# A two-block transformer on one core: the 32 small experts of the last layer get 21 load buffers, a plain fp32 gather and a reordered last stretch

## The chip, the core and the metric

The kernel runs on one core of a Trainium2 chip. The metric is device microseconds of one launch, median of several runs. The clock of TensorE (PE) is granted in two levels, 2.4 and 1.2 GHz; the column PEclk of the views is the mean of a stretch as a share of the higher one. SP is the engine that issues nearly all loads from HBM.

## The reference, cut to what matters

256 tokens of width 1024 pass two blocks. The first has sliding-window attention with a feed-forward net, then a forgetting attention with an 8-expert layer. The second has a hybrid mixer and a hierarchical layer of 32 experts, each between a residual and a layer norm. The change lies in the second block, for the most part in its expert layer:

```python
x = layer_norm_2(DEEPNORM_ALPHA * x + hybrid_mixer(x, ...), ln1_w[l], ln1_b[l])
h = hier_moe(x, router_group_w[l], ..., expert_w_gate[l], expert_w_up[l], expert_w_down[l])
x = layer_norm_2(DEEPNORM_ALPHA * x + h, ln2_w[l], ln2_b[l])

def hier_moe(x, ...):          # 4 groups of 8 experts, the best 2 of the best group
    g_logits = xf @ router_group_w + router_group_b
    g_sel = jnp.argmax(g_logits, axis=-1)
    e_logits = (xf @ router_expert_w + router_expert_b).reshape(T, 4, 8)[g_sel]
    top_logit, top_local = lax.top_k(e_logits, 2)
    weight = p_group * jax.nn.softmax(top_logit, axis=-1)
    ...
    hid = silu(xb @ expert_w_gate[e]) * (xb @ expert_w_up[e])
    y[tok] += (hid @ expert_w_down[e]) * weight
```

Each expert has three matrices of 1024 x 256 in fp32, 1 MB each, so the layer reads 96 MB.

## The kernel before, in words

**The end of the mixer** (`hybrid`, L2333). Its last dense pieces are the projection `up(0)` of the RWKV branch (L2513 adds its product to `hm`), the transposes of `hm` with a split into `xh` and `xl`, and the product with `w_out`, done by `out_gemm` in four pairs of 512 KB loads. Dense weights come by L107 (`k.st`) into tiles `wr`; ScalarE (L123) and VectorE (L124) then split each into two fp32r parts in buffers `ws`. How many split buffers there are at that place is set by `room(0, 3, ...)`: six. Then the layer norm, and `moe2`.

**The loads of the experts** (`Long`, `k.long2`, L191). A load takes the buffer that was used longest ago, and is issued in the order gate, up, down of each group of four experts: twelve loads of 1 MB a group, eight groups. The last four down matrices are split into eight halves, so there are 100 loads. SP issues all of them in program order; hardware loads have eight semaphores, so at most eight are under way, and a further one waits for the oldest. Buffers: `LONG2 = (5, 8)` of its own, five before `w_out` and eight after it, and four tiles of the mixer that are dead by then (`rpar`, `hy0`, `hy1`, `rz`): 17 in all. The first nine loads are issued between the second and the third load of `w_out`, the next eight once the mixer's pools close.

**The expert layer** (`moe2`). The router (L2552 loads `xwr`) ranks and counts; L2623 (`places_of`) makes the one-hot matrix `OH` of 32 slots an expert. `gather(q)` collects the tokens of two groups at once: 32 matmuls of 256 columns, in fp32r, with `x` in a high and a low part (`xxth`, `xxtl`; L2594 subtracts). Then an `If` (L2663, L2664) stands for experts with more than 32 tokens; with this input it isn't taken. On every engine it is a branch, and SP's path around it waits until each of the eight load semaphores has come. Then, for each q of 8: gate matmuls (128x32 outputs, `bank_g<-wx,xgx`), `combine` of the group before (`bank_acc<-xy,xOT`), up matmuls, the product `xhid` (L2725), its transposes, down matmuls, and `xy` (L2753, L2754). At q = 0, `slot_gates` stands between gate and up. At q odd, `gather(q + 1)` follows the up matmuls. At q = 5, L2733 issues two loads that spread the norm vectors over all partitions (512 KB each). At q = 7 the residual (four fp32 matmuls of 512 columns into `bank_acc`, from an `x` that ScalarE had multiplied by alpha at L2662) stands between up and down. The down matmuls of q = 7 come in two column halves, each with its own `xy`, `combine` and statistics.

Of the kernel before, what the change touches and what calls it, by code (L numbers as in the profile page):

```python
# [158 lines left out]
class Long:  # L159
# [20 lines left out]
    def load(self, kept=0):  # L180

        while self.done < len(self.plan):
# [10 lines left out]
            self.done += 1  # L193

# [263 lines left out]
def out_gemm(k, key, hi, lo, order, ln, ready=(), need={}, last=4):  # L458
# [3 lines left out]
    for grp in [[q] for q in order[:-last]] + [order[-last:]]:  # L462
        yield from until(ready, *(need[q] for q in grp if q in need))
        final = grp[-1] == order[-1]
        ws = [w[0] for w in k.st.get(*((key, q) for q in grp), *(ln.keys if final else ()))]
        if final:
            ln.take(ws[-2:])
# [21 lines left out]
def leftover(k, x, xT, over, n, kf, up, down):  # L489
# [3 lines left out]
    with k.pool("rest") as pool, tc.For_i(0, n) as e:  # L493
        acc = [[k.bank("acc") for _ in range(2)] for _ in range(2)]
        for j in range(kf):
            ps = [k.t()[:, :T] for _ in range(2)]
            for p, src in zip(ps, up(e, j)):
                for a in range(0, KD, 4):
                    w = pool.tile([128, 4, 128], F32, name="ow", tag="ow", bufs=1)
                    nc.sync.dma_start(w, src[:, a:a + 4])  # L500
                    for q in range(4):
                        k.pe.matmul(p, w[:, q], xT[:, a + q], start=a + q == 0, stop=a + q == KD - 1)
            h = pool.tile([128, T], F32, name="oh", tag="oh", bufs=1)
            nc.scalar.activation(h, ps[0], AF.Silu)
            nc.vector.tensor_mul(h, h, ps[1])
            for m in range(2):
                v = pool.tile([128, 512], F32, name="ow", tag="ow", bufs=1)
                nc.sync.dma_start(v, down(e, j)[:, m * 512:m * 512 + 512])
                for tb in range(2):
                    k.pe.matmul(acc[tb][m], h[:, tb * 128:tb * 128 + 128], v, start=j == 0, stop=j == kf - 1)  # L510
        for tb in range(2):
            for m in range(2):
                r = x[:, tb, m * 512:m * 512 + 512]
                nc.vector.scalar_tensor_tensor(r, acc[tb][m], over[:, tb, ds(e, 1)], r, op0=OP.mult, op1=OP.add)
# [724 lines left out]
def moe1(k, A, x, alpha, before, br):  # L1239
# [3 lines left out]
    with ExitStack() as mo:  # L1243
# [8 lines left out]
        with ExitStack() as ro:  # L1252
# [85 lines left out]
            with tc.If(nv > CAP):  # L1338
                wi, wo = (A[n].rearrange("l e a b -> (l e) a b") for n in ("w_exp_in", "w_exp_out"))
                leftover(k, x, xT, over, NE, KF,  # L1340
                         lambda e, j: [wi[ds(e, 1), :, i * DFF + j * 128:i * DFF + j * 128 + 128].rearrange(
                             "o (k p) n -> (o p) k n", p=128) for i in range(2)],
                         lambda e, j: wo[ds(e, 1), j * 128:j * 128 + 128].rearrange("o p n -> (o p) n"))
# [989 lines left out]
def hybrid(k, A, x, before, scratch, extra):  # L2333
    nc, tc = k.nc, k.tc
    with ExitStack() as hy:
# [7 lines left out]
        r = Rwkv(k, A, yp, wide)  # L2343
        ready = set()
# [8 lines left out]
        with ExitStack() as pa:  # L2353
# [42 lines left out]
            def dense():  # L2396
# [4 lines left out]
                for i in range(3):  # L2401
                    yield from mb(1, i)
                late = iter(())
# [27 lines left out]
        with ExitStack() as pb:  # L2431
# [34 lines left out]
            def dense2():  # L2466
# [30 lines left out]
                yield from gate(0, gt)  # L2497
# [19 lines left out]
            og = out_gemm(k, "o2", xh, xl, list(range(8)), ln)  # L2517
# [21 lines left out]
def moe2(k, A, x, alpha, bias, out):  # L2539
    nc, tc = k.nc, k.tc  # L2540
    with ExitStack() as mo:
# [4 lines left out]
        OH = pool.tile([128, 2, NX, CAP2], F32R, name="xOH")  # L2546
        gate = pool.tile([128, 8], F32, name="xgate")
        own = pool.tile([128, 4], F32, name="xown")
        xth, xtl = (pool.tile([128, 2, D], F32R, name=n, tag=n, bufs=1) for n in ("xxth", "xxtl"))
        wr = pool.tile([128, KD, 4 + NX], F32, name="xwr")  # L2550
        for nm, a, n in (("group", 0, 4), ("expert", 4, NX)):
            nc.sync.dma_start(wr[:, :, a:a + n], dram(A[f"router_{nm}_w_2"], 0, [[n, 128], [128 * n, KD], [1, n]]))  # L2552
        k.long2.load()
        mo.enter_context(k.banks(g=2, t=2, acc=4))
        gx = pool.tile([128, KD, 256], F32, name="xgx")

        def gather(q):

            for a in range(0, KD, 2):
                p = k.t()  # L2560
                for j in range(a, a + 2):
                    for i, src in enumerate((xth, xtl)):
                        for tb in range(2):
                            w = src[:, tb].rearrange("p (c j) -> p j c", j=KD)[:, j]
                            k.pe.matmul(p[:, (j - a) * 256:(j - a) * 256 + 256], w,
                                        OH[:, tb, 4 * q:4 * q + 8].rearrange("p e s -> p (e s)"),
                                        start=i == 0 and tb == 0, stop=i == 1 and tb == 1)
                k.copy(gx[:, a:a + 2], p.rearrange("p (j s) -> p j s", j=2))

        with ExitStack() as ro:  # L2570
            rp = ro.enter_context(k.pool(name="m2r", bufs=1))
            tl = lambda shape, name: rp.tile(shape, F32, name=name)
            xT = tl([128, KD, T], "xxT")
# [5 lines left out]
            ln = LayerNorm(k, x, 1.0, "nx")  # L2579
            for tb in range(2):  # L2580
                if tb == 0:
                    nc.scalar.copy(xth[:, 0], x[:, 0])
                turn_half(k, x, xT, tb)
                if tb:
                    nc.scalar.copy(xth[:, 1], x[:, 1])
# [6 lines left out]
                if tb:  # L2592
                    for i in range(2):
                        nc.vector.tensor_sub(xtl[:, i], x[:, i], xth[:, i].bitcast(F32))  # L2594
# [32 lines left out]
            places_of(0, 8)  # L2627
# [5 lines left out]
            places_of(8, NX)  # L2633
# [27 lines left out]
            for tb in range(2):  # L2661
                nc.scalar.mul(x[:, tb], x[:, tb], alpha)  # L2662
            nv = nc.values_load(cnt[0:1, 0:1], min_val=0, max_val=T)  # L2663
            with tc.If(nv > CAP2):  # L2664
# [201 lines left out]
```

## Time and profile before

| | |
|---|---|
| median of 3 runs | 1883.89 us (1883.79 to 1885.23) |
| profiled execution | 1883.33 us, of which span 1881.6 us |
| PE busy | 92% of the span |
| mean granted clock | 0.966 |
| DMA | 515.95 MB, 274 GB/s mean |

The difference of 1.73 us between the profiled execution and its span lies around the span and is taken as fixed. The last 300 us, the end of the mixer and the expert layer, are read in stretches of 5 and of 20 us; the shares of the whole span say little about them.

### The profile page before, as it was taken

What the parts mean: (1) busy time and instruction counts of PE and PEld (TensorE: products, weight loads), DVE (VectorE), ACT (ScalarE), POOL (GpSimd) and SP (SyncE); (2) the same over time, 40 slices, a digit from 0 to 9 for tenths busy, and PEclk for the clock granted to TensorE, in tenths of its full rate; (3) what the DMA queues carried; (4) which work ended last, traced back from release to release, by engine and by line L of the source; (5) the groups of instructions that cost most, each with busy time, mean ns of one, the idle gap of its engine ahead of it and who ended that gap; (6) DMA issues with size and microseconds to landing.
All of it is one profiled execution on the core that took longest, in us unless ns stands there. A gap on an engine that the chain in (4) does not pass through costs nothing. (4 is left out here: it accounts for less than half of the span.)

```text
span 1881.6 us, 41532 instructions
## 1 busy us (share of the span) xinstructions
PE 1735.6 (92%) x18447; PEld 1199.3 (64%) x18447; DVE 721.0 (38%) x1147; ACT 453.4 (24%) x791; POOL 364.9 (19%) x621
## 2 busy tenths in 40 slices
PE   8989999899899999999999999989989998798676
PEld 7867888788645464646565555678767676564242
DVE  5557664654502020210202020357676666511102
ACT  5534444364200000000000101033353333221000
POOL 5410999310100000000000000064333331000000
PEclk9999999999999999999999999989999999999988
DMA  7515666535499999999999999755464236789996
GB/s 224 152 58 182 203 234 200 178 101 199 184 348 384 405 385 401 385 401 388 385 405 372 417 370 415 263 198 156 133 181 123 85 97 220 286 341 419 419 419 251
DMA packets 126478, 515.95 MB, mean 274 GB/s; under 512 B 20892, under 2 KB 49994, under 8 KB 88916
## 3 DMA queue, kind: packets, MB, share of 16 engines
q1 hardware_dynamic: 123012, 497.39, 70.4%
q0 software_dynamic: 3280, 15.83, 2.5%
q8 instruction: 147, 2.41, 0.5%
q14 instruction: 39, 0.32, 0.1%
HBM read 503.48 MB, written 7.87 MB: 272 GB/s over the span
## 5 line engine op out<-in xcount | busy, mean ns | idle before, releaser
L223 PE MATMUL bank_r<-wl,gx 128*32 128x352 f32 x6144 | 459.4, 460 | 2.6 <-ACTq L1338 2.6
L223 PE MATMUL bank_g<-ws,xh 128*128 128x256 f32 (+2 forms) x1440 | 392.0, 353 | 17.7 <-ACT ws L123 8.6
L223 PEld LDWEIGHTS bank_r<-wl,gx 128*32 128x32 f32 x6144 | 220.5, 110 | 234.8 <-issue 125.2
L124 DVE TENSOR_TENSOR ws<-wr,ws 128x1024 fp32r<-128x1024 f32 (+1 forms) x200 | 258.0, 1300 | 162.1 <-ACT ws L123 161.7
L223 PEld LDWEIGHTS bank_g<-ws,xh 128*128 128x128 f32 x1440 | 259.4, 197 | 58.0 <-ACT ws L123 9.5
L123 ACT ACTIVATE ws<-wr 128x1024 fp32r<-128x1024 f32 (+1 forms) x200 | 209.6, 1057 | 212.6 <-PE bank_g L223 108.8
L223 PE MATMUL bank_g<-ws,xl 128*128 128x256 f32 (+2 forms) x720 | 237.7, 346 | 3.6 <-DVE xl L354 3.4
L223 PE MATMUL bank_r<-wl,ehT 128*32 128x256 f32 x4224 | 231.4, 379 | 4.2 <-DVE ehT L1425 4.0
L223 PEld LDWEIGHTS bank_r<-wl,ehT 128*32 128x32 f32 x4224 | 161.2, 110 | 72.2 <-issue 8.9
L1424 DVE TENSOR_TENSOR eh<-eh,bank_r 128x352 f32<-128x352 f32 x48 | 22.9, 505 | 428.4 <-PE bank_r L223 427.8
L547 POOL TENSOR_TENSOR lnmv<-lnmv,neghalf 128x1 f32<-128x1 f32 x10 | 10.0, 998 | 828.1 <-DVE lnmv L546 828.1
L223 PEld LDWEIGHTS bank_g<-ws,xl 128*128 128x128 f32 x720 | 142.1, 197 | 18.5 <-DVE xl L354 5.2
L1447 ACT CAST ey<-bank_r 128x256 fp32r<-128x256 f32 x24 | 8.9, 373 | 415.4 <-PE bank_r L223 414.5
L223 PE MATMUL bank_g<-wx,xgx 128*32 128x256 f32 x784 | 78.6, 429 | 21.1 <-DMA wx<-in_expert_w_gate_dram 14.0
L1448 DVE TENSOR_TENSOR ey<-bank_r,ey 128x256 fp32r<-128x256 f32 x24 | 10.1, 424 | 165.0 <-ACT ey L1447 164.9
L1418 ACT ACTIVATE eh<-bank_r 128x352 f32<-128x352 f32 x48 | 22.3, 465 | 206.8 <-PE bank_r L223 201.7
L223 PEld LDWEIGHTS bank_g<-wx,xgx 128*32 128x32 f32 x784 | 35.7, 122 | 52.6 <-DMA wx<-in_expert_w_gate_dram 18.3
L631 POOL TENSOR_TENSOR aP<-aP,ast 128x512 f32<-128x512 f32 (+1 forms) x20 | 24.9, 1243 | 173.6 <-DVE ast L629 132.4
L223 PE MATMUL bank_g<-ws,hh 128*128 128x512 f32 x176 | 57.5, 399 | 0.0
L223 PE MATMUL bank_g<-ws,oh 128*128 128x512 f32 x128 | 44.5, 410 | 0.0
L1425 DVE STREAM_TRANSPOSE ehT<-eh 128x704 f32<-128x704 f32 x24 | 43.0, 1791 | 0.8
L564 POOL TENSOR_TENSOR lnmv<-lnmv,neghalf 128x1 f32<-128x1 f32 x2 | 1.1, 560 | 215.1 <-DVE lnmv L563 215.1
(714 smaller groups left out, 2230.2 us busy)
## 6 DMA issues: line engine op xcount, KB each, us to landing
wl<-in_w_exp_in_dram SPq DMA_DIRECT2D x128, 1408.0 KB, 8.7
wl<-in_w_exp_out_dram SPq DMA_DIRECT2D x64, 1408.0 KB, 8.5
wr<-in_w_in_dram SPq DMA_DIRECT2D x54, 512.0 KB, 3.9
wx<-in_expert_w_gate_dram SPq DMA_DIRECT2D x26, 1024.0 KB, 19.1
wx<-in_expert_w_up_dram SPq DMA_DIRECT2D x23, 1024.0 KB, 19.9
wr<-in_w_ffn_in_dram SPq DMA_DIRECT2D x44, 512.0 KB, 4.4
wx<-in_expert_w_down_dram SPq DMA_DIRECT2D x21, 1024.0 KB, 19.9
wr<-in_w_out_dram SPq DMA_DIRECT2D x24, 512.0 KB, 4.2
```

Of the source, the lines that this page charges most:

```text
L123: nc.scalar.activation(hv, v, AF.Copy)
L124: nc.vector.tensor_sub(lv, v, hv.bitcast(F32))
L223: self.nc.tensor.matmul(out, lhsT, rhs, start=start, stop=stop)
L547: nc.gpsimd.tensor_tensor(mv[:, 3:4], mv[:, 2:3], self.k.neghalf, op=OP.pow)
L564: nc.gpsimd.tensor_tensor(mv[:, 3:4], mv[:, 2:3], self.k.neghalf, op=OP.pow)
L631: e.tensor_mul(P[:, hs, :nk], P[:, hs, :nk], st[:, 3, hs].rearrange("p (h o) -> p h o", o=1).to_broadcast([128, 2, nk]))
L1418: nc.scalar.activation(h[:, g, s * H2:s * H2 + H2], pa[g][s], AF.Silu)
L1424: nc.vector.tensor_mul(v, v, pb[g][s])
L1425: nc.vector.transpose(hT[:, g], h[:, g].rearrange("p (r j) -> p j r", j=KF))
L1447: nc.scalar.copy(y[:, 0, g], ps[g])
L1448: nc.vector.tensor_sub(y[:, 1, g], ps[g], y[:, 0, g].bitcast(F32))
```

## The change

Buffers and the order of loads: `LONG2 = (1, 8, 8)`. One own buffer exists from the mixer's start and takes its load among those of `w_in`. Two tiles (`hy1`, `hy0`) take theirs in the middle of `gate(0)`, before the loads of `w_up_rwkv`. Then `rpar`, `rz` and eight own buffers come, one load for each call of `more()`, between the loads of `w_out`; eight more follow at the end of the mixer. That is 21. Split buffers at `w_out`: four (`room(0, 1, ...)`).

```diff
-            extra(k.part_y, wide, ("rpar", "hy0", "hy1", "rz"))
+            spare(wide, "rpar", "rz")
+            more = extra(k.part_y)
...
                     mm3(k, p, [(br[0][:, 2 * q + j, ts], br[1][:, 2 * q + j, ts], ws[2 * n + q][0][:, j], ws[2 * n + q][1][:, j])
                                for q in range(2) for j in range(2)], True, True)
+                    more()
...
-LONG2 = (5, 8)
+LONG2 = (1, 8, 8)
...
+        def extra(until):
+            k.long2.room(LONG2[1])
+            held.append(room(0, 1, until))
+
+            def more():
+                k.st.load()
+                k.long2.load(most=1)
+            more()
+            return more
```

On SP's queue, from the first load of `w_out` on (`wr<-in_w_out`), before; `wx`, `hy`, `rpar` and `rz` are buffers of expert loads:

```order
L107 DMA wr_15614<-in_w_out_dram 128x1024
L107 DMA wr_15631<-in_w_out_dram 128x1024
L191 DMA wx_15664<-in_expert_w_gate_dram 128x2048
L191 DMA wx_15666<-in_expert_w_gate_dram 128x2048
L191 DMA wx_15668<-in_expert_w_gate_dram 128x2048
L191 DMA wx_15670<-in_expert_w_gate_dram 128x2048
L191 DMA wx_15672<-in_expert_w_up_dram 128x2048
L191 DMA rpar<-in_expert_w_up_dram 128x2048
L191 DMA hy_15676<-in_expert_w_up_dram 128x2048
L191 DMA hy_15678<-in_expert_w_up_dram 128x2048
L191 DMA rz<-in_expert_w_down_dram 128x2048
L107 DMA wr_15687<-in_w_out_dram 128x1024
```

The same place now:

```order
L107 DMA wr_15623<-in_w_out_dram 128x1024
L107 DMA wr_15640<-in_w_out_dram 128x1024
L192 DMA rpar<-in_expert_w_gate_dram 128x2048
L192 DMA rz<-in_expert_w_up_dram 128x2048
L192 DMA wx_15677<-in_expert_w_up_dram 128x2048
L107 DMA wr_15684<-in_w_out_dram 128x1024
L107 DMA wr_15689<-in_w_out_dram 128x1024
L192 DMA wx_15704<-in_expert_w_up_dram 128x2048
L192 DMA wx_15721<-in_expert_w_up_dram 128x2048
L192 DMA wx_15745<-in_expert_w_down_dram 128x2048
L192 DMA wx_15769<-in_expert_w_down_dram 128x2048
L107 DMA wr_15787<-in_w_out_dram 128x1024
```

Nine expert loads stood between the second and third load of `w_out`; now three do, and four between the fourth and fifth.

The gather and what goes with it: `xp` holds `x` in plain fp32, permuted so that the weights of a gather are contiguous (two ScalarE copies in place of the two casts). `gather(q)` runs for each q, with 16 matmuls of 128 columns. The subtractions of L2594 and the multiplication of L2662 are gone; `places_of` makes the first four experts, not eight, ahead of `gather(0)`.

```diff
-            for a in range(0, KD, 2):
+            for a in range(0, KD, 4):
                 p = k.t()
-                for j in range(a, a + 2):
-                    for i, src in enumerate((xth, xtl)):
-                        for tb in range(2):
...
+                for j in range(a, a + 4):
+                    for tb in range(2):
+                        k.pe.matmul(p[:, (j - a) * 128:(j - a) * 128 + 128], xp[:, tb, j],
+                                    OH[:, tb, 4 * q:4 * q + 4].rearrange("p e s -> p (e s)"), start=tb == 0, stop=tb == 1)
...
             if q < 7:
-                if q % 2:
-                    gather(q + 1)
...
+                gather(q + 1)
+            if q == 6:
+                rest()
                 for tb in range(2):
                     for n in range(2):
-                        k.pe.matmul(acc[tb][n], k.ident, x[:, tb, n * 512:n * 512 + 512], start=False, stop=False)
+                        k.pe.matmul(acc[tb][n], identa, natural(tb)[:, 64 * n:64 * n + 64], start=False, stop=False)
```

`rest()` is the branch for experts with more than 32 tokens, now at q = 6; the residual follows it, with alpha in the identity `identa`. The norm vectors come as 32 bytes a partition each (`xrows`, two loads of 4 KB); at q = 7, between gate and up, 16 matmuls of 128 columns with four copies spread them over a spare expert buffer. `xhid`, `xhT` and `xOT` have one buffer, not two. The descriptor area of the software queue is set to 4096 bytes (`dynamic_dma_scratch_size=4096`).

On SP's queue, the end of the expert stream before (the `hy` and `rz` of 512 columns are halves of down matrices; the names with `out` are the store of the result):

```order
L191 DMA hy_17265<-in_expert_w_up_dram 128x2048
L191 DMA hy_17267<-in_expert_w_down_dram 128x2x512
L191 DMA rz<-in_expert_w_down_dram 128x2x512
L191 DMA wx_17312<-in_expert_w_down_dram 128x2x512
L191 DMA wx_17314<-in_expert_w_down_dram 128x2x512
L191 DMA wx_17316<-in_expert_w_down_dram 128x2x512
L191 DMA wx_17339<-in_expert_w_down_dram 128x2x512
L191 DMA wx_17341<-in_expert_w_down_dram 128x2x512
L191 DMA wx_17343<-in_expert_w_down_dram 128x2x512
L583 DMA out_dram<-x 128x512 x4
```

Now, up to the branch:

```order
L192 DMA wx_17081<-in_expert_w_up_dram 128x2048
L192 DMA wx_17083<-in_expert_w_down_dram 128x2x512
L192 DMA wx_17134<-in_expert_w_down_dram 128x2x512
L192 DMA wx_17136<-in_expert_w_down_dram 128x2x512
L192 DMA wx_17138<-in_expert_w_down_dram 128x2x512
L192 DMA wx_17140<-in_expert_w_down_dram 128x2x512
L2692 TENSOR_LOAD xcnt
L2692 ISA x2
L2694 COMPARE_AND_BRANCH
```

The branch stands on SP between the fifth and the sixth half; the last three halves follow behind its body.

## Rows read from the trace of the kernel before

**Rows 1.** Windows: us, busy by engine (instructions), PEclk, DMA share, GB/s.
```profile
1700.00:1720.00 20.00, 13.10 (x119) 4.88 (x121) 2.35 (x4) 1.96 (x3) 0.00 (x0) 0.92 1.01 418
1680.00:1880.00 200.00, 148.90 (x1226) 76.68 (x1218) 27.94 (x46) 18.52 (x32) 4.63 (x6) 0.90 0.93 383
```
**Rows 2.** Chain of waits in the expert layer: start, length, what.
```profile
1663.18 4.91 PE bank_g L223 x64
...
1694.92 19.24 DMA wx<-in_expert_w_gate_dram
...
1833.06 19.90 DMA hy<-in_expert_w_up_dram
1853.01 5.33 PE bank_g L223 x58
1858.33 3.63 PE bank_acc L223 x8
...
1867.13 1.90 PE bank_g L223 x16
```
**Rows 3.** Windows of 5 us around w_out and the first gate group.
```profile
1609.00:1614.00 5.00, 3.59 (x8) 2.39 (x9) 3.58 (x3) 4.13 (x5) 0.00 (x0) 0.50 0.59 209
1649.00:1654.00 5.00, 4.85 (x49) 4.21 (x52) 2.57 (x5) 1.93 (x3) 0.83 (x4) 1.00 0.38 154
```
**Rows 4.** Timeline of SP: start, length of issuing, instructions, count.
```profile
1589.89 23.31 SPq L107 DMA_DIRECT2D wr<-in_w_out_dram  x6
...
1632.85 24.24 SPq L191 DMA_DIRECT2D wx<-in_expert_w_up_dram  x4
...
1804.18 0.33 SPq L2733 DMA_DIRECT2D xxth<-in_ln_w_dram  x1
```
**Rows 5.** Timelines of DVE, ACT and PE around w_out: [idle before, and its releaser].
```profile
1583.51 4.63 DVE L124 TENSOR_TENSOR ws<-wr,ws 128x1024 fp32r<-128x1024 f32 x4 [1.65 <-ACT ws L123]
1609.27 1.06 ACT L123 ACTIVATE ws<-wr 128x1024 fp32r<-128x1024 f32 x1 [10.37 <-DMA wr<-in_w_out_dram]
1589.61 0.63 PE L227 MATMUL bank_t<-ident,hm 128*128 128x128 f32 x4 [2.95 <-DVE hm L2513]
1589.99 4.59 PE L223 MATMUL bank_g<-ws,hyr 128*128 128x512 f32 x12
1594.78 3.06 PE L223 MATMUL bank_g<-ws,hyr 128*128 128x512 f32 x12
1610.37 0.79 PE L223 MATMUL bank_g<-ws,xh 128*128 128x512 f32 x1 [5.81 <-ACT ws L123]
```
**Rows 6.** Timeline of PE: router, gather(0), first gate, slot_gates, the combine in q = 7.
```profile
1631.53 1.94 PE L223 MATMUL bank_g<-xxT,xwr 128*36 128x128 f32 x16
...
1644.04 0.73 PE L223 MATMUL bank_t<-xOH,xxth 128*128 128x256 f32 x2 [1.13 <-DVE xOH L2623]
...
1652.16 3.66 PE L223 MATMUL bank_g<-wx,xgx 128*32 128x256 f32 x64
1656.89 5.33 PE L223 MATMUL bank_t<-xG,xOH 128*128 128x4 f32 x32 [1.08 <-POOL xG L2659]
...
1848.25 2.14 PE L223 MATMUL bank_acc<-xy,xOT 128*128 128x512 f32 x8
```
**Rows 7.** DMA issues: count, KB each, median us from issue to landing.
```profile
wr<-in_w_in_dram SPq DMA_DIRECT2D x54, 512.0 KB, 3.9
...
sCX<-far POOLq DMA_DIRECT2D x2, 1280.0 KB, 8.7
```
**Rows 8.** The two branch lines: engine, operation, duration ns, first and last start.
```profile
L1338 PEldq COMPARE_BRANCH  x1: 3918/3918/3918, 510.5 to 510.5; - x1
L2664 SPq EVENT_SEMAPHORE  x8: 17/17/17, 1652.9 to 1653.4; - x8
```
**Rows 9.** Timeline of POOL: the last of six loads issued in a row, and its use.
```profile
1247.35 0.54 POOL L1628 DMA_DIRECT2D sm<-far  x1
1249.94 1.60 POOL L1752 COPY srho<-sm 128x512 f32<-128x512 f32 x1 [2.05 <-DMA sm<-far]
```

More of the change, by code (lines that the diff above doesn't have):

```diff
@@ L178, in add, with load @@
         self.plan.append((dram(w, off, [[pitch, 128], *rows]), part))
-    def load(self, kept=0):
-        while self.done < len(self.plan):
+    def load(self, kept=0, most=1 << 30):
+        until = min(self.done + most, len(self.plan))
+        while self.done < until:
             b = min(self.bufs, key=lambda b: b[2])
@@ L486, in out_gemm, with leftover @@
                     ln.add(tb, n, ps[tb][n])
-def leftover(k, x, xT, over, n, kf, up, down):
+def leftover(k, x, xT, over, n, kf, up, down, tile, tbs=(0, 1), tag="acc"):
     nc, tc = k.nc, k.tc
-    with k.pool("rest") as pool, tc.For_i(0, n) as e:
-        acc = [[k.bank("acc") for _ in range(2)] for _ in range(2)]
+    with tc.For_i(0, n) as e:
+        nt = 128 * len(tbs)
+        acc = [[k.bank(tag) for _ in range(2)] for _ in tbs]
         for j in range(kf):
-            ps = [k.t()[:, :T] for _ in range(2)]
+            ps = [k.t()[:, :nt] for _ in range(2)]
             for p, src in zip(ps, up(e, j)):
                 for a in range(0, KD, 4):
-                    w = pool.tile([128, 4, 128], F32, name="ow", tag="ow", bufs=1)
+                    w = tile(512, "ow").rearrange("p (k n) -> p k n", k=4)
                     nc.sync.dma_start(w, src[:, a:a + 4])
                     for q in range(4):
-                        k.pe.matmul(p, w[:, q], xT[:, a + q], start=a + q == 0, stop=a + q == KD - 1)
-            h = pool.tile([128, T], F32, name="oh", tag="oh", bufs=1)
+                        k.pe.matmul(p, w[:, q], xT[:, a + q, tbs[0] * 128:tbs[0] * 128 + nt],
+                                    start=a + q == 0, stop=a + q == KD - 1)
+            h = tile(nt, "oh")
             nc.scalar.activation(h, ps[0], AF.Silu)
@@ L2343, in hybrid @@
         r = Rwkv(k, A, yp, wide)
+        k.long2.room(LONG2[0])
         ready = set()
@@ L2402, in dense @@
                     yield from mb(1, i)
+                k.long2.load()
                 late = iter(())
@@ L2496, in dense2 @@
                     yield from up(1, n, *bm)
-                yield from gate(0, gt)
+                for i, _ in enumerate(gate(0, gt)):
+                    if i == 2:
+                        spare(wide, "hy1", "hy0")
+                    yield
             weave(k, dense2(), r.steps(*br), r.ahead(room), lat=LAT_B)
@@ L2545, in moe2 @@
         G = pool.tile([128, 2, NX], F32, name="xG")
-        OH = pool.tile([128, 2, NX, CAP2], F32R, name="xOH")
+        OH = pool.tile([128, 2, NX, CAP2], F32, name="xOH", tag="xOH", bufs=1)
+        rows = pool.tile([128, 2, KD], F32, name="xrows")
         gate = pool.tile([128, 8], F32, name="xgate")
         own = pool.tile([128, 4], F32, name="xown")
[L2549 to L2553, printed above, removed]
+        xp = pool.tile([128, 2, KD, 128], F32, name="xp")
+        ordered = lambda tb: x[:, tb].rearrange("p (c j) -> p j c", j=KD)
+        natural = lambda tb: xp[:, tb].rearrange("p j c -> p c j")
         mo.enter_context(k.banks(g=2, t=2, acc=4))
-        gx = pool.tile([128, KD, 256], F32, name="xgx")
+        gx = lambda q: x[:, q % 2].rearrange("p (j s) -> p j s", j=KD)
         def gather(q):
-            for a in range(0, KD, 2):
+            for a in range(0, KD, 4):
                 p = k.t()
-                for j in range(a, a + 2):
-                    for i, src in enumerate((xth, xtl)):
[L2563 to L2568, printed above, removed]
+                for j in range(a, a + 4):
+                    for tb in range(2):
+                        k.pe.matmul(p[:, (j - a) * 128:(j - a) * 128 + 128], xp[:, tb, j],
+                                    OH[:, tb, 4 * q:4 * q + 4].rearrange("p e s -> p (e s)"), start=tb == 0, stop=tb == 1)
+                k.copy(gx(q)[:, a:a + 4], p.rearrange("p (j s) -> p j s", j=4))
         with ExitStack() as ro:
@@ L2572, in moe2 @@
             tl = lambda shape, name: rp.tile(shape, F32, name=name)
+            wr = tl([128, KD, 4 + NX], "xwr")
+            for nm, a, n in (("group", 0, 4), ("expert", 4, NX)):
+                nc.sync.dma_start(wr[:, :, a:a + n], dram(A[f"router_{nm}_w_2"], 0, [[n, 128], [128 * n, KD], [1, n]]))
+            for i, nm in enumerate("wb"):
+                nc.sync.dma_start(rows[:, i], dram(A[f"ln2_{nm}_2"], 0, [[KD, 128], [1, KD]]))
+            k.long2.load()
             xT = tl([128, KD, T], "xxT")
```

110 lines of the change are left out of this document (67 added, 43 removed).

## The prediction

> **What bounds the kernel now.** I read the windows of the expert layer first, then the chain of waits, then windows of 5 us back to where the loads begin, then the timelines of SP and of the computing engines there. In the expert layer the transfers are the bound: from 1700 to 1720 us the DMA share is 1.01 at 418 GB/s, and PE is busy 148.9 of the 200 us from 1680 on [rows 1]. The chain says the same: from 1694.92 to 1853.01 it is one expert load after another, eight pieces, each about 19.9 us long [rows 2]. With eight loads under way that is 19.9 / 8 = 2.5 us for 1 MB. So whatever brings a load forward by 2.5 us, or takes 1 MB out of the stream, brings the end forward, as long as nothing else becomes late.
>
> The stream isn't full all the time. From 1649 to 1654 the DMA share is 0.38 [rows 3]. All 17 buffers are full there: SP begins its last four issues at 1632.85 and isn't through with them for 24.24 us [rows 4], since a buffer is free again only when the first gate matmuls end, at 1652.16 + 3.66 = 1655.8 [rows 6]. Two things therefore set the place of the stream: how much has landed when the first group releases buffers, and when that is. That time is set by the mixer's end. There the rows show four losses. PE waits 2.95 us for `hm`, because DVE is busy from 1583.51 for 4.63 us with splits of `w_out` that nobody needs yet. PE waits 5.81 us at 1610.37, since ACT waited 10.37 us for a `w_out` load, to 1609.27 [rows 5]; that load stood in SP's queue behind nine expert loads, and six loads took 23.31 us to issue [rows 4]. And after each wait the clock is low: 12 matmuls take 4.59 us, where the next 12 take 3.06 (1.5 us lost) [rows 5], and the window from 1609 has a granted clock of 0.50, the 1.2 GHz level [rows 3], where 3.59 us go into eight matmuls; I put that at about 2.0 us. Sum: 2.95 + 5.81 + 1.5 + 2.0 = 12.3 us.
>
> **The change, part by part.**
>
> *Order at `w_out`.* Three expert loads stand ahead of the third `w_out` load, not nine: 6 x 2.5 = 15 us less queue, more than the 5.81 us of waiting. With four split buffers in place of six, DVE has two splits fewer ahead of `hm`, half of 4.63 us, so 2.3 of the 2.95 us go and most of the rest with them. New waits come: a split may now only start when PE has read the buffer's last content. One conversion and its subtraction, 1.06 + 4.63 / 4 = 2.2 us [rows 5], lie open once, and I add 0.7 us for a second partly hidden one. So -12.3 + 2.9 = -9.4 us. Ends: none open, -12.3; each of the three later pairs open as far as its 2.2 us plus 0.3 of slow clock, -12.3 + 7.5 = -4.8.
>
> *The first gather.* Before, it runs from 1644.04 to 1652.16, 8.1 us, for two groups. Now 16 matmuls for one group. The nearest low row is the router's, fp32 with 128 columns: 1.94 us for eight (16 records), 0.243 each, so 3.9 us; but its weights have 36 columns. `slot_gates` has weights of 128 and 4 columns at the low clock, 5.33 / 16 = 0.33 us each [rows 6]; with 128 columns instead and all at the low clock I bound it by the sum, 0.33 + 2 x 0.243 = 0.82, so 13 us. I take 6.2 us, between and near the low end, as the clock is high when the gather begins: -1.9. The one-hot matrix for four experts and not eight and the missing subtraction give another -0.4. Ends: -4.6 and +4.5. Together with `w_out`: -11.7 us at the first release (1655.8 becomes 1644.1) and, with the same matmuls up to there, at the end of the first up matmuls (1663.18 + 4.91 = 1668.1 [rows 2] becomes 1656.4).
>
> *Buffers.* At the first release 21 loads have landed instead of 17: they end about 20 us (eight loads) after the mixer's pools close, which is before 1644. Four loads of the stream are gone from the time after it: 4 x 2.5 = -10.0 us. Working from the front: four more land by about 1657, 71 MB are left, 71 x 2.5 = 177.5 us; the last byte lands near 1835 to 1837.
>
> *Norm vectors.* The two spread loads, the first at 1804.18 in the full stream [rows 4], carry 1 MB: -2.5 us. Two loads of 4 KB early cost nothing that anyone waits for.
>
> *Early loads.* The one among the `w_in` loads and the two ahead of `w_up_rwkv` can delay a dense load behind them by 2.5 to 5 us. A dense load lands in 3.9 us [rows 7], and splits wait in buffers ahead of PE, so I take 0; the other end is +2.5.
>
> *The tail.* The end before is 1881.6 - 1853.01 = 28.6 us behind the last up load (call that landing L). The residual leaves it: -3.63 us [rows 2]. In exchange 16 row matmuls stand ahead of the last up matmuls, 6.2 us like the gather's 16; they begin when `combine` ends, at 1848.25 + 2.14 = 1850.4 [rows 6], 2.6 us before L. So the up matmuls start 3.6 us later, but with no wait ahead of them they run as the group at 1652.16 does, 3.66, not 5.33 us. The second half of the down matmuls then wants to start at 1867.13 - 1853.01 = 14.1, minus 3.6, plus 3.6, minus 1.7: L + 12.4. Its weights come hardly sooner: SP's way round the branch waits for all eight semaphores, as the eight events of L2664 show before [rows 8], and only then issues three halves. The fifth half lands at about L + 5.2, the first of the three 3.9 us later [rows 7], the others 1.2 us apart: L + 11.5, within an us. So PE is last, at 12.4, and from there to the end it is 1881.6 - 1867.13 = 14.5 us as before: 26.9 instead of 28.6, -1.7 us. With the row matmuls at the low clock (6.2 us more) it would be +4.5.
>
> *At q = 6* the branch, the gather and the residual stand between up and down. The other branch of this form, L1338, cost PE 3.9 us [rows 8]; with 6.2 and 3.6 us that is 13.7 us beside a period of 12 x 2.5 = 30 us, of which PE uses about 22 (148.9 / 200 of it). Some 8 us are hidden, and the down buffers have the reserve of four more loads, 10 us. I take 0, and +5 as the other end.
>
> *The small area* for software descriptors I take at 0; its other end is rival 3.
>
> Sum: -9.4 - 2.3 - 10.0 - 2.5 - 1.7 = -25.9. From the profiled execution, 1883.33 us, which is 0.6 us under the median: **1857.4 us**.
>
> The Trainium skill, "DMA: Bandwidth & Descriptors", section "Specifications", gives about 358 GB/s as what HBM gives one core, which would be 2.9 us for 1 MB. The trace doesn't agree, with 418 GB/s over a whole window; by the page the five saved megabytes would be worth 14.6 us, not 12.5, and the sum -28.0. The measured rate stands.
>
> **Rivals.**
>
> 1. *`w_out` gains nothing.* Four split buffers put ACT, DVE and PE in line, and what the queue gives back is lost at the splits. For it: each of the four pairs needs two conversions and two subtractions, 4.5 us, not far from PE's own work on a pair, 24 matmuls of 3.06 / 12 us [rows 5], 6.1 us. Against: they run beside it as long as a buffer is free. Then -16.5: 1866.8 us.
>
> 2. *The work at q = 6 and the row matmuls are on the path.* PE has a slow clock in waits, the branch costs more than 3.9, and the release of buffers slips: +5, and 6.2 in the tail: 1868.6 us.
>
> 3. *Slower: the software queue.* POOL issues six loads in a row from 1244.60, the last at 1247.35, and the second of them is used 2.05 us later [rows 9]. If the smaller area holds one at a time, POOL waits for a landing between each two: 5 x 6.3 = 31.5 us, with 6.3 between the two landings of [rows 7]. It decides above 25.9 us, so nearly all of it would have to reach the end. Then 1857.4 + 31.5 = 1888.9. For it: POOL works half of that stretch and others wait for it. Against: no row shows POOL waiting for room, and 128 pieces a load are little.
>
> The Trainium skill has the area at 16 KiB a partition ("SBUF — State Buffer", section "SBUF size: 192, 224, or 256?") and nine descriptors a side and engine for 1 MiB, of 16 bytes ("DMA: Bandwidth & Descriptors", sections "The descriptor swizzle" and "Terms"); an estimate from that is 6 x 9 x 16 = 864 bytes for the six, inside 4096. No run here shows it.
>
> 4. *It doesn't do what it says.* The stream begins earlier but some later wait pins it, for instance buffers that PE releases too late for 21 to help; the new gather after each up at q even (6 us more there) could do that. Then only small gains remain, some 3 us: 1880.
>
> **How the numbers follow.** Forecast 0.58, its own range 1850 to 1865 (the ends of `w_out` and of the gather, not both at once). Rival 1 0.17, rival 2 0.11, rival 3 0.08, rival 4 0.06. The range 1850 to 1870 takes in the forecast and rivals 1 and 2; it leaves out rivals 3 and 4 and 0.05 of the others. A measurement of this kernel tells 0.2%, 3.8 us, from no change. Faster: 0.58 + 0.17 + 0.11 = 0.86. Within: rival 4, 0.06. Slower: 0.08.
>
> **What would show it.** PE's wait before `hm` and the 5.81 us at the first `w_out` pair gone, and the end of the `w_out` matmuls near 1620 (1629 before). First gate matmuls ending near 1644, `gather(0)` of 5 to 7 us. DMA share 1.0 from about 1657 to 1835. Eight semaphore events of SP in the last 25 us, then three halves; the residual ahead of the last group. It is wrong if the end of `w_out` stays near 1629 (rival 1), if PE is late with down at q = 6 (rival 2), if the start of the mixer moves (rival 3), or if the DMA share has holes after 1660 (rival 4).

## The result

The changed kernel takes 1860.88 us (median of 4 runs, 1858.82 to 1866.05), the kernel before 1883.84 us; the ratio is 0.9882, with a 95% interval of 0.986 to 0.9905. That is 23.0 us less; 25.9 us less were forecast, and the time lies inside the range of 1850 to 1870.

The profiled execution took 1866.05 us, the longest of the four, with a span of 1864.3 us. Where that matters below, the profile of a kernel that differs in its last three loads alone (`e2_loads_first`) stands beside it.

### The profile page after: what moved, and what is told of

Same layout as the page of the kernel before. It is cut to its first block, busy times and chain, and to the rows that moved or that the text cites. A ratio compares the mean times of both kernels' runs of the same rounds, so it can differ in the third digit from the quotient of the medians.

```text
span 1864.3 us, 41874 instructions
## 1 busy us (share of the span) xinstructions
PE 1730.8 (93%) x18607; PEld 1197.5 (64%) x18607; DVE 718.0 (39%) x1147; ACT 455.7 (24%) x791; POOL 363.9 (20%) x622
## 5 line engine op out<-in xcount | busy, mean ns | idle before, releaser
L232 PEld LDWEIGHTS bank_r<-wl,ehT 128*32 128x32 f32 x4224 | 161.2, 110 | 72.2 <-issue 8.9
L232 PE MATMUL bank_g<-wx,x 128*32 128x256 f32 x784 | 71.2, 433 | 15.6 <-DMA wx<-in_expert_w_gate_dram 14.4
L232 PEld LDWEIGHTS bank_g<-wx,x 128*32 128x32 f32 x784 | 32.7, 123 | 45.6 <-DMA wx<-in_expert_w_gate_dram 19.1
```

The source lines that it names most:

```text
L232: self.nc.tensor.matmul(out, lhsT, rhs, start=start, stop=stop)
```

## The profile after

**End of the mixer and first loads.** The timeline of SP, which answers to [rows 4]: start, length of issuing, count.

```profile
1578.08 1.47 SPq L107 DMA_DIRECT2D wr<-in_w_out_dram  x2
...
1585.15 1.46 SPq L107 DMA_DIRECT2D wr<-in_w_out_dram  x2
...
1597.69 3.74 SPq L107 DMA_DIRECT2D wr<-in_w_out_dram  x4
...
1627.60 19.71 SPq L192 DMA_DIRECT2D wx<-in_expert_w_down_dram  x2
```

The third `w_out` load goes out at 1585.15, and the last four need 3.74 us; before, six needed 23.31 us. The timelines of PE and DVE there, which answer to [rows 5]:

```profile
1583.89 2.36 DVE L124 TENSOR_TENSOR ws<-wr,ws 128x1024 fp32r<-128x1024 f32 x2 [1.65 <-ACT ws L123]
```
```profile
1587.72 0.63 PE L236 MATMUL bank_t<-ident,hm 128*128 128x128 f32 x4 [0.68 <-DVE hm L2540]
1588.11 3.04 PE L232 MATMUL bank_g<-ws,hyr 128*128 128x512 f32 x12
...
1596.45 0.50 PE L232 MATMUL bank_g<-ws,xh 128*128 128x512 f32 x1 [1.63 <-ACT ws L123]
...
1597.71 1.02 PE L232 MATMUL bank_g<-ws,xh 128*128 128x512 f32 x2 [0.53 <-DVE ws L124]
...
1622.98 0.60 PE L236 MATMUL bank_t<-ident,x 128*128 128x128 f32 x4
```

DVE has two splits ahead of `hm`, not four; the wait for `hm` is 0.68 us instead of 2.95, and the 12 matmuls behind it take 3.04 instead of 4.59. The wait of 5.81 us is gone. New are 1.63 and 0.53 us at the first `w_out` pair: the split buffers are still in use, as the text had charged. The transposes at 1622.98 mark the end of the `w_out` matmuls; before, they stood at 1629.16.

**First group and the hole in the stream.** PE's timeline of the changed kernel, then of `e2_loads_first`: `gather(0)` and `slot_gates`, which answer to [rows 6].

```profile
1637.94 5.44 PE L232 MATMUL bank_t<-xOH,xp 128*128 128x128 f32 x32 [0.86 <-DVE xOH L2651]
...
1648.32 6.24 PE L232 MATMUL bank_t<-xG,xOH 128*128 128x4 f32 x32 [1.35 <-POOL xG L2687]
```
```profile
1640.43 3.81 PE L232 MATMUL bank_t<-xOH,xp 128*128 128x128 f32 x32 [0.86 <-DVE xOH L2651]
...
1649.18 3.73 PE L232 MATMUL bank_t<-xG,xOH 128*128 128x4 f32 x32 [1.35 <-POOL xG L2687]
```

The same instructions take 5.44 and 6.24 us in the one execution, 3.81 and 3.73 us in the other. The granted clock differs with them. Windows of the changed kernel, then of `e2_loads_first`: columns as in [rows 1], PEclk third from the end.

```profile
1639.00:1644.00 5.00, 5.00 (x41) 4.62 (x43) 2.84 (x5) 0.53 (x1) 0.30 (x2) 0.66 1.02 423
1644.00:1649.00 5.00, 3.65 (x62) 2.22 (x55) 0.23 (x2) 3.77 (x9) 2.58 (x12) 1.00 0.44 143
1649.00:1654.00 5.00, 5.00 (x27) 5.00 (x26) 0.00 (x0) 0.00 (x0) 0.29 (x1) 0.52 0.99 411
1654.00:1659.00 5.00, 5.00 (x43) 2.82 (x47) 1.07 (x3) 0.00 (x0) 0.00 (x0) 0.50 0.92 387
1659.00:1664.00 5.00, 5.00 (x63) 3.87 (x56) 0.42 (x1) 0.59 (x1) 0.00 (x0) 0.96 0.37 116
```
```profile
1640.00:1645.00 5.00, 4.57 (x48) 4.20 (x52) 3.18 (x6) 0.65 (x2) 0.00 (x0) 1.00 1.01 419
1645.00:1650.00 5.00, 3.65 (x64) 2.25 (x52) 0.55 (x6) 3.65 (x8) 3.01 (x13) 1.00 0.76 280
1650.00:1655.00 5.00, 5.00 (x47) 3.98 (x50) 1.07 (x3) 0.00 (x0) 0.15 (x1) 0.80 1.02 424
1655.00:1660.00 5.00, 5.00 (x69) 3.12 (x62) 0.42 (x1) 0.00 (x0) 0.00 (x0) 0.86 0.95 385
```

In the changed kernel's profile the granted clock is 0.66 during the gather and 0.52 and 0.50 from 1649 to 1659, the 1.2 GHz level; in the other it is full during the gather. PE idles 1.35 us ahead of `slot_gates` in both, so that stretch alone doesn't explain the difference, and no run shows what does. In the ten other profiles that have the new gather, `gather(0)` takes 3.81 us: the changed kernel's own profile is the exception.

The holes in the stream, a DMA share of 0.44 and 0.37, answer to the 0.38 of [rows 3]. They are still there with 21 loads landed, the first one 5 us earlier. With the full clock they are small: 0.76, then 0.95.

**The tail.** PE's timeline, which answers to the end of [rows 2]:

```profile
1815.57 7.25 PE L232 MATMUL bank_acc<-xp,xidenta 128*128 128x512 f32 x8 [4.66 <-PEq L2694]
...
1832.62 1.95 PE L232 MATMUL bank_t<-ident,xrows 128*128 128x128 f32 x16
1834.84 2.05 PE L232 MATMUL bank_t<-ident,xrows 128*128 128x128 f32 x16 [0.27 <-ACT xgb L332]
...
1848.17 1.05 PE L232 MATMUL bank_g<-wx,xhT 128*32 128x512 f32 x2 [0.56 <-DMA wx<-in_expert_w_down_dram]
1849.48 1.90 PE L232 MATMUL bank_g<-wx,xhT 128*32 128x512 f32 x10 [0.27 <-DMA wx<-in_expert_w_down_dram]
```

The last transfer in the chain of waits (start, length):

```profile
1842.36 7.08 DMA wx<-in_expert_w_down_dram
```

The two branch rows that answer to [rows 8]:

```profile
L2694 SPq EVENT_SEMAPHORE  x8: 17/17/17, 1837.9 to 1840.9; - x8
L2694 PEldq COMPARE_BRANCH  x1: 6032/6032/6032, 1809.2 to 1809.2; - x1
```

PE idles 4.66 us behind the branch, the residual takes 7.25 us where it took 3.63, and the up matmuls start right behind the row matmuls, with no wait for weights. SP is through with its eight events at 1840.9. The first three of them, at 1837.9, 1839.2 and 1840.5, stand until the third, fourth and fifth half have landed (1837.8, 1839.2 and 1840.5); the other five follow within 0.4 us. Then SP issues the last three halves, at 1841.00, 1841.71 and 1842.36; the last of them lands 7.1 us later, and PE's last down matmuls wait for it to 1849.48.

## A yardstick for the runs

Between executions the whole program shifts: the first 12-matmul piece of `up(0)` starts at 1580.00 before and 1580.11 after, but anywhere from 1575.5 to 1584.0 in the eleven profiles that have the new order. Times of single stages are therefore counted from that start, and the tail from the issue of the first half load, which the stream alone sets (eight loads are under way, so it goes out when an earlier load lands).

| profile | up(0) starts | end of w_out | first gate | end of first up | first half issued | end, from that issue |
|---|---|---|---|---|---|---|
| before | 1580.00 | +49.2 | +72.2 | +88.1 | +255.5 | 46.1 |
| after | 1580.11 | +42.9 | +63.2 | +80.9 | +236.3 | 47.9 |
| e2_loads_first | 1583.97 | +41.5 | +60.2 | +74.6 | +229.9 | 45.2 |
| e3_17_buffers | 1580.47 | +41.4 | +60.1 | +74.5 | +239.6 | 48.3 |
| e7_loads_in_a_row | 1578.08 | +53.0 | +71.7 | +86.0 | | |

All of it is worked out from the timelines of PE and SP. The changed kernel's row has the low clock of its own profile in it. How far a single profile can be trusted in the last column, programs with the same or nearly the same tail show: the two variants of the kernel before (without its branch, and with the small descriptor area) have 44.5 us there, not 46.1, and the changed kernel and the five variants that keep its tail have 46.7 to 48.3. The first two rows of the last two columns give the result of the profiled executions: -19.2 up to the first half, +1.8 behind it, +0.1 ahead of `up(0)`, -17.3 in all, the difference of the spans.

## The experiments

**The branch left out.**

```diff
             if q == 6:
-                rest()
```

> The changed kernel without the branch at q = 6: the path for experts with more than 32 tokens is left out, all else stays. Theory A (PE is late at the end, because of the 4.66 us that it idles behind the branch and of a residual of 7.25 us at the low clock just behind it, and the three last halves are late by SP's way round the branch): the up matmuls of q = 7 wait for their weights again, the residual takes about 3.7 us, the last halves are there when the second half of the down matmuls starts; 5 to 8 us less than the changed kernel, 1853 to 1856. Theory B (the work at q = 6 is hidden behind the stream and only the late halves cost): 3 us less, about 1858.

1855.88 us (ratio 0.9837, 0.9812 to 0.9862), 5 us under the changed kernel. PE's timeline shows that the residual stayed long:

```profile
1807.98 7.10 PE L232 MATMUL bank_acc<-xp,xidenta 128*128 128x512 f32 x8
...
1820.70 0.40 PE L232 MATMUL bank_g<-rpar,x 128*32 128x256 f32 x1 [0.72 <-DMA rpar<-in_expert_w_gate_dram]
```

The window of the residual, columns as in [rows 1]:

```profile
1808.00:1815.00 7.00, 7.00 (x11) 1.71 (x10) 0.00 (x0) 0.59 (x1) 0.00 (x0) 1.00 1.01 421
```

With a granted clock of 1.00 it takes 7.10 us, and 7.25 in the changed kernel with 0.70, so the low clock was not the reason, against theory A. What differs from the residual before is the read: `natural(xp)` steps 128 elements from column to column, where `x` was contiguous. The weights are new as well (`identa` in place of the plain identity), and no run separates the two. The rest went as A has it: with the 4.66 us gone, PE waits again (0.72 us) at the gate of q = 7, and the end comes 42.9 us after the issue of the first half, not 47.9.

**The last halves ahead of the branch.**

```diff
             if q == 6:
+                k.long2.load()
                 rest()
```

> The changed kernel with its last three half loads issued ahead of the branch on SP, nothing else. Both theories: the second half of the down matmuls no longer waits; it started at 1849.48 and PE was through with the work before it at 1847.6, and it ran with gaps; 2 to 3 us less, 1858 to 1859. If the halves weren't the last thing waited for: no change.

1859.92 us (0.9874, 0.9841 to 0.9907). The medians don't separate 1 us; the profile does: the end is 45.2 us behind the first half's issue instead of 47.9, and no wait for a half is left in PE's timeline. So SP's way round the branch costs 2.7 us by this pair of profiles, 1.5 to 3.1 against all six with that tail (46.7 to 48.3).

**17 buffers.**

```diff
-LONG2 = (1, 8, 8)
+LONG2 = (1, 8, 4)
...
-                    gb = k.long2.spare([128, 2, D], "xgb")
+                    gb = ep.tile([128, 2, D], F32, name="xgb")
```

> The changed kernel with 17 buffers (four own ones fewer at the last stage) and a tile of its own for the spread norm vectors, so that only the buffers differ. Theory A: four loads of 1 MB come back into the stream behind the first release, 4 x 2.5 = 10 us, of which the 3.5 us that PE was late at the last up matmuls absorb a part: 6 to 10 us more, 1867 to 1871. Theory C (the gain is the earlier first release alone, buffers don't matter): no change.

1870.35 us (0.9937, 0.9912 to 0.9962), 9.5 us over the changed kernel. The stage up to the first gate is the same as with 21 (+60.1 and +60.2), and the first half is issued at +239.6 instead of +229.9: 9.7 us for four loads, 2.4 each (8.3 to 10.2 us against `e2_loads_first` and the four other variants with 21 buffers that keep the loads in between and the residual at q = 6). Theory C falls, and the lateness of PE absorbs nothing that shows. One more thing differs: with 17 buffers the branch stands on SP between the first and the second half, so seven halves go out behind it, not three; the last column of the table, 48.3 us, hardly shows it.

**Six split buffers.**

```diff
-LONG2 = (1, 8, 8)
+LONG2 = (1, 6, 10)
...
-            held.append(room(0, 1, until))
+            held.append(room(0, 3, until))
```

> The changed kernel with six split buffers at w_out, as before, and the buffers of the experts as six there and ten after it, 21 as in the changed kernel. Theory A: PE's 1.63 and 0.53 us of waiting at the first w_out pair and the low clock behind them (about 2.5 us) go, but DVE has four splits ahead of hm again (2.3 us): the end of the w_out matmuls near 1621 instead of 1623, 0 to 2 us less in all. If the split buffers are what made the gain at w_out smaller than forecast: 4 us less.

1860.53 us (0.9886, 0.9855 to 0.9917): no change.

```profile
1585.20 0.63 PE L236 MATMUL bank_t<-ident,hm 128*128 128x128 f32 x4 [2.95 <-DVE hm L2540]
```

(Two of the experts' own buffers also come later in this kernel.) The wait of 2.95 us for `hm` is back to the hundredth, and the 1.63 and 0.53 us at the first pair are gone; the end of `w_out` is at +41.1 instead of +41.5. The two numbers of split buffers trade one wait for another.

**Loads in a row at `w_out`.**

```diff
             def more():
                 k.st.load()
-                k.long2.load(most=1)
+                k.long2.load()
```

> The changed kernel with the ten expert loads at w_out issued in a row, between its second and third load, as before; buffers, split buffers and all else as changed. Theory A (the interleaving is what shortens the end of the mixer): the third w_out load stands behind 10 MB again, 25 us; PE waits 6 to 9 us in the middle of w_out and has the low clock after it, the end of the w_out matmuls is 7 to 10 us later and with it the end: 1866 to 1870. Theory F (the fewer splits ahead of hm did it, the transfers are hidden): no change.

1869.01 us (0.9926, 0.9897 to 0.9955), 8.1 us over the changed kernel. In PE's timeline:

```profile
1611.24 0.80 PE L232 MATMUL bank_g<-ws,xh 128*128 128x512 f32 x1 [7.83 <-ACT ws L123]
```

The stall before, 5.81 us, returns as 7.83, with ten loads ahead of `w_out` where there were nine. The end of `w_out` is at +53.0 instead of +41.5. So the interleaving makes the end of the mixer shorter; theory F falls.

**The residual spread over q = 2 to 5**, with the halves first. The branch's body clears `xp` and adds the residual of its own results.

```diff
-                for tb in range(2):
-                    for n in range(2):
-                        k.pe.matmul(acc[tb][n], identa, natural(tb)[:, 64 * n:64 * n + 64], start=False, stop=False)
...
+            if 2 <= q <= 5:
+                tb, n = (q - 2) // 2, q % 2
+                k.pe.matmul(acc[tb][n], identa, natural(tb)[:, 64 * n:64 * n + 64], start=False, stop=False)
```

> The changed kernel with the three last halves issued ahead of the branch, and the residual not at q = 6 but one matmul at each of q = 2 to 5, where PE waits for weights (the branch's body then adds only what the overflow changes). Theory A (at the end PE is late by what stands at q = 6): against the kernel with the halves first alone, PE is 7.1 us less late behind the branch and then waits for the gate weights of q = 7; 2 to 3 us less, 1857 to 1858, with up matmuls that still follow the row matmuls. Theory D (the residual was hidden): no change against 1860.

1854.03 us (0.9842, 0.9809 to 0.9875).

```profile
1808.48 0.67 PE L236 MATMUL bank_t<-ident,xhid 128*128 128x128 f32 x2 [4.73 <-PEq L2694]
...
1816.81 0.40 PE L232 MATMUL bank_g<-rpar,x 128*32 128x256 f32 x1 [0.45 <-DMA rpar<-in_expert_w_gate_dram]
```

The branch still costs PE 4.73 us, but PE now waits for the gate weights, so the branch is hidden. The end lies 43.1 us behind the first half's issue, 2.1 less than with the halves first alone. Theory D falls: 2 us of the work at q = 6 were on the path. The median moved by more than the profile, 5.9 us, which the spread of the runs (1848.83 to 1857.88) covers.

**Front and tail together.** In addition, the row matmuls go ahead of the gate matmuls of q = 7, and at q = 0 `slot_gates()` and `back(0)` go behind the up matmuls.

```diff
-                    if q == 0:
-                        slot_gates()
-                    if q % 2 == 0:
+                    if q and q % 2 == 0:
                         back(q)
...
             nc.vector.tensor_mul(hid, hid, ph[:, FX:])
+            if q == 0:
+                slot_gates()
+                back(0)
```

> As the kernel before it in this list, and the row matmuls ahead of the gate matmuls of q = 7 (PE waits there), and slot_gates and the transposes of the one-hot matrix at q = 0 behind the up matmuls instead of ahead of them. Theory A: the first up matmuls end some 6 us earlier, so the hole in the stream while the buffers are full shrinks by 3 to 5 us; the row matmuls leave the end, another 2 us: 1851 to 1854. Theory E (the stream's place is set by the first release of the gate buffers alone): 2 us less than the kernel before it.

1854.84 us (0.985, 0.9825 to 0.9875): no better than the kernel before it. The first half goes out 2.4 us sooner (+229.1 against +231.5), but the tail stays at 43.1 us. Theory E was nearer: the hole is small when the clock is full, as its windows from 1640 to 1645 show a share of 0.76, and none behind. This one and the kernel with the spread residual have the lowest medians of all that keep the path for full experts, 6 to 7 us under the changed kernel; their intervals still touch its own.

**A second branch**, at q = 3, with a short body and with a long one.

```diff
                 gather(q + 1)
+            if q == 3:
+                nv = nc.values_load(cnt[0:1, 0:1], min_val=0, max_val=T)
+                with tc.If(nv > CAP2):
+                    nc.gpsimd.tensor_scalar(own, own, 1.0, None, op0=OP.mult)
```

> The changed kernel with one more branch that isn't taken, at q = 3 in the full stream, with a body of one POOL instruction. If the 6.0 us that PE's branch instruction takes at q = 6 come from the length of the body it jumps over (instructions to be fetched): well under 1 us at q = 3. If they come from the full transfer queues (a fetch behind 8 MB): about 6 us again. SP's way round it lets eight loads land and begins anew: a hole of 2 to 3 us in the stream either way, so 2 to 3 us more in all.

> The changed kernel with a second branch at q = 3 as in the run with the short body (PE's branch instruction took 0.23 us there), but a body of 88 transposes on PE, about as many matmuls as the body at q = 6 has. If the 6.0 us at q = 6 are the length of what is jumped over: 4 to 6 us at q = 3 now. If they belong to the place (the last group, or loops inside the body): under 1 us again.

The rows of the branch's line: PE's instruction at q = 3, with the short body and then with the long one (88 transposes more):

```profile
L2781 PEldq COMPARE_BRANCH  x1: 234/234/234, 1717.8 to 1717.8; - x1
```
```profile
L2781 PEldq COMPARE_BRANCH  x1: 344/344/344, 1714.1 to 1714.1; - x1
```

0.23 and 0.34 us, in a full stream both times. At q = 6 the same instruction takes 6.0 us in the first program, as in eight others, but 1.6 us in the second, where PE idles only 0.30 us behind it:

```profile
1805.82 1.95 PE L232 MATMUL bank_acc<-xp,xidenta 128*128 128x512 f32 x2 [0.30 <-PEq L2694]
```

So 88 matmuls jumped over don't make the 6 us, nor does a full queue alone. The traces hold a better candidate: the packets of 16 KB on the queue that the page calls instruction (`q8`). In all 14 traces every long branch of PE, at q = 6 and at the place of L1338, ends 1.3 to 1.6 us behind the end of such a packet; in the changed kernel the packet runs from 1812.74 to 1813.82 and the branch to 1815.26. At the four short ones (0.23 to 0.36 us) the last such packet had ended 8 us before. And the queues do count for the length: in the nine of 6.0 us at q = 6, with a DMA share of 1.01 in the changed kernel, the packet waited for starts 5.3 to 5.8 us behind the one before it; at the place of L1338, with 0.32, 2.4 to 3.3 us. This points to PE waiting for its next instructions; no run separates what makes one branch need a packet and another not. The tail is 47.1 us even where PE's branch is short, so PE's own wait was not the last one there: SP's loads were. SP shows no semaphore events at q = 3, where the bodies issue no loads; the hole of 2 to 3 us that I had expected of it didn't come. The times were 1862.87 and 1859.40 us, one run each.

**Before, without its branch.** The lines from `nv = ...` to the end of the `If` in `moe2` are taken out.

```diff
-            nv = nc.values_load(cnt[0:1, 0:1], min_val=0, max_val=T)
-            with tc.If(nv > CAP2):
...
```

> The kernel before without its branch (the path for experts with more than 32 tokens is left out). Theory A (all 17 buffers are full where SP goes round the branch, so its waiting costs nothing but the 1.4 us between the freeing of the buffers at 1655.8 and the next issue at 1657.2): 0 to 1.5 us less than before. Theory G (a part of the gain of the change is that the branch left the place ahead of the first gate): 3 us less or more.

1882.82 us, ratio 0.9997 (0.9982 to 1.0011): no change. At its old place the branch was hidden behind full buffers; theory G falls. So the move of the branch gained nothing at the front, and at its new place the branch costs 5 us (the first run of this list).

**Before, with the small descriptor area.**

```diff
-    nc = bacc.Bacc("TRN2", target_bir_lowering=False, num_devices=1)
+    nc = bacc.Bacc("TRN2", target_bir_lowering=False, num_devices=1, dynamic_dma_scratch_size=4096)
```

> The kernel before with the descriptor area of the software queue at 4096 bytes, nothing else. Forecast: no change. Rival 3 of the prediction: POOL's six loads in a row at 1244 us no longer follow each other within 0.6 us, and the time grows by several us.

Ratio 1.0005 (0.9993 to 1.0017): no change. POOL's timeline, which answers to [rows 9]:

```profile
1243.15 0.54 POOL L1628 DMA_DIRECT2D sm<-far  x1
1245.97 1.40 POOL L1752 COPY srho<-sm 128x512 f32<-128x512 f32 x1 [2.28 <-DMA sm<-far]
```

The first of the six went out at 1240.38: the sixth still follows within 2.8 us. Rival 3 falls.

**Spread loads in place of row matmuls**, with 17 buffers.

```diff
+                if q == 5:
+                    gb = ep.tile([128, 2, D], F32, name="xgb")
+                    ln.g, ln.b = gb[:, 0], gb[:, 1]
+                    for t, nm in ((ln.g, "w"), (ln.b, "b")):
+                        nc.sync.dma_start(t, dram(A[f"ln2_{nm}_2"], 0, [[0, 128], [1, D]]))
```

> The kernel with 17 buffers of the first series (1870.35 us), with the norm vectors spread by two loads of 512 KB issued at q = 5, as before, in place of the 16 row matmuls and their copies. By the prediction's terms: the stream has 1 MB more, +2.5 us, and PE has 4.1 us less ahead of the last up matmuls, which are then bound by their weights: -1 to +2.5 us.

1871.98 us (0.9943, 0.992 to 0.9965), 1.6 us over the kernel with 17 buffers, within both intervals. The first half goes out at +242.0 instead of +239.6: the 1 MB costs 2.4 us of the stream. PE then waits for its weights at q = 7 (0.69 and 1.88 us), so it gains little from the 4 us that it no longer spends on row matmuls.

## Why the prediction was right, and where it was off

All in us; "after" is the changed kernel's profile, "e2" that of `e2_loads_first`, both against the profile before.

| step | forecast | measured |
|---|---|---|
| end of `w_out` | -9.4 | -6.3 after, -7.7 in e2 |
| with the first gather, at the first gate | -11.7 | -9.0 after, -12.0 in e2 |
| at the end of the first up matmuls | -11.7 | -7.2 after, -13.5 in e2 |
| four buffers | -10.0 | 9.7 (first half), 9.5 (time), 17 against 21 |
| norm vectors out of the stream | -2.5 | 2.4 |
| stream from first up to first half | -12.5 | -12.0 after, -12.1 in e2 |
| tail | -1.7 | +1.8 after, -0.9 in e2 |
| work at q = 6 | 0 (to +5) | about +2 (e2 against the spread residual), part of the tail's |

**What bounds the kernel** was read rightly: the stream sets the end, and a megabyte is worth 2.4 us, by buffers (2.1 to 2.6 over the profiles) and by spread loads alike. That stream term, half of the sum, came within 0.5 us.

**The order at `w_out`.** Right in kind, as the run with the loads in a row shows, and sized a fifth (e2) to a third (after) too high. Counted piece by piece in the changed kernel's profile, the first pair took 3.9 us more than before, where 2.9 were charged; the wait for `hm` gave back 2.0 us, not 2.95; and the stretch with the old stall of 5.81 us gave 6.7 us, not 7.8, since short waits for splits (0.28 and 0.29 us) are new there.

**The first gather.** No run changes it alone, so this is read from the timelines: 3.81 us at the high clock, 0.24 for each matmul, the row of the router and the low end of the bound; 6.2 was taken, so this term gained 2 us more than forecast wherever the clock was high. The profiled execution ends the first up matmuls 6.3 us later than e2 (80.9 against 74.6): 1.4 of it lie ahead of the end of `w_out`, 1.6 in the stretch with the gather, 3.3 in `slot_gates` and the up matmuls. The prediction had carried the clock in its bounds for the gather alone, and took the two behind it to be the same before and after. They were 1.7 us longer in the one profile and 1.6 us shorter in the other; that the sum fits between is luck with the clock.

**The tail** is the step that failed, inside the bounds given (+4.5, and +5 for the work at q = 6). Count as the prediction does, from L, the landing of the last up load: 1852.96 before, 1833.83 after. The end came at L + 30.5, not 26.9; before, it was L + 28.7, and L + 27.0 in the two variants of the kernel before, whose last up matmuls ran at the full clock. PE's own part was right: the up matmuls start at L + 3.0 (3.6 forecast) and take 3.64 us (3.66), and the second half of down could start at L + 12.7 (12.4). But the last half, put at L + 11.5, lands at L + 15.6. Three terms of that sum were too small: the fifth half lands at L + 6.7, not 5.2 (the trace of the kernel before has 6.8 for it); the first of the three 4.9 us behind it, not 3.9; the last another 4.1 us later, not 2.4. With the halves ahead of the branch, in e2, the last lands at L + 10.7 and nothing waits for it.

The work at q = 6, put at nothing, cost about 2 us, by the spread residual: four matmuls that took 3.63 us before take 7.25, and PE idles 4.66 us behind the branch. The row matmuls, charged at 6.2 us, took 4.2 and hid a part of that.

**What is luck.** In `e2_loads_first` and the four other variants with 21 buffers that keep the loads in between and the residual at q = 6, all with the full clock in `gather(0)`, L lies 24.3 to 26.1 us earlier than before, counted from `up(0)`; 24.2 were forecast. With 25.4 (e2) and a tail that is 1.9 us longer, the sum is -23.5, near the -23.0 of the medians. So the forecast came within 2.9 us because its two misses, 1.2 us too little for the front and 3.6 too little for the tail, have opposite signs; and the four runs alone spread over 7 us.

**The rivals.** Rival 1 had the right mechanism for a part of the shortfall at `w_out` (splits in line), not its size. Rival 2 is what happened in small. Rival 3 didn't occur. The sign given for rival 4, a hole after 1660, did show (0.37 from 1659 to 1664), but the share is 1.01 from 1664 on, and the time of 1880 didn't come.

## What to carry to other kernels

In a stretch that a stream of loads bounds, a free buffer is worth about the time of its load (2.1 to 2.6 us for 1 MB here), as long as the buffers are full at the first release; and a load that is issued early is best issued between the loads that the present stage needs, not ahead of them. A branch that isn't taken cost nothing where all buffers were full, and 5 us in front of the last loads: issue what is still to come ahead of it. Work that is moved to where an engine waits is free only up to that wait, so price the moved form (here a residual with a stepped read and new weights, at twice the time), not the form that stood there before. And read a stage from more than one execution: two profiles of the same code up to there, at different granted clocks, end the first group 6 us apart.

## What the runs showed of the hardware that I had not expected

- The four residual matmuls of 512 fp32 columns take 3.63 us with a contiguous operand, and 7.10 us with one that steps 128 elements and a scaled identity as weights, at a granted clock of 1.00; with 0.70 they take 7.25, so the clock hardly matters to that form. One alone takes 1.90 us. No run separates the step from the weights.
- PE's branch instruction takes 0.23 to 0.36 us at some places, 3.3 to 3.9 at L1338, and at q = 6 6.0 to 6.3 us in nine profiles and 1.6 in one. Every long one ends 1.3 to 1.6 us behind the end of a 16 KB packet on the instruction queue.
- The start of `up(0)` varies by 8.5 us between executions of programs that are alike up to there, more than most effects of a single edit; stages have to be counted from a mark of their own.
